# Gate tables summed by adding DMAs instead of one-hot products, in a PEER layer kernel

## The chip, the cores and the metric

One core of a Trainium2 chip runs the kernel. The metric is the device time of one execution in microseconds, from the first to the last instruction on the slowest core (there is only one). Less is better.

## What is computed

One layer of a streaming encoder on 256 tokens of width 2048, in float32: a mixer (chunked attention, a gated short convolution, gates), a cross attention, and a PEER feed-forward, each behind an RMSNorm and added to the residual, and a last norm. The change is in the PEER part:

```python
q = (h @ w_pq).reshape(bsz, seq, PEER_HEADS, 2, PEER_HALF)
s = jnp.einsum('bshpd,hpkd->bshpk', q, sub_keys)
s1, i1 = lax.top_k(s[:, :, :, 0], PEER_TOPK)          # 16 of 128 keys, 8 heads
s2, i2 = lax.top_k(s[:, :, :, 1], PEER_TOPK)
cand = s1[..., :, None] + s2[..., None, :]             # 256 candidates
top_s, pos = lax.top_k(cand, PEER_TOPK)                # expert = i1 * 128 + i2
gates = jax.nn.softmax(top_s, axis=-1)
# per token, over 8 x 16 chosen experts e of 16384:
#   out += gelu(h . expert_u[e]) * gate * expert_v[e]
```

Several heads of one token may choose the same expert; their gates then add up.

## The kernel before

Every product of the kernel streams a weight matrix in 1 MB pieces, the **tiles** of this text (`order`, in `plan`). SyncE loads a piece (`raw`, 2 buffers, line 162), ScalarE rounds it to its high half (`whi`, line 175), VectorE subtracts to get the low half (`wlo`, line 183), and TensorE multiplies both halves (`gemm_f`, lines 279 and 282). `take` fetches the halves of a tile and starts the next loads; after each tile `run_side` (line 202) hands out side work in the order in which it will stand on the engines: entries of `bulk` up to a credit of 2.75 us per tile, then the tile's `wlo`, then one entry of `chain`, then all of `late`. All engines work their instructions in this order, so what stands ahead of a `wlo` on VectorE, or ahead of a `raw` load on SyncE, holds it back.

PEER runs so. During `w_pq` (16 tiles) the key scores are made (line 1047) and `key_top` picks 16 keys, for both blocks of 128 tokens in turn. During `expert_u` (128 tiles, 16384 experts) the activations h . expert_u go to a DRAM table `ag_d` (and `tail_d` for the last 512 experts), and beside it the routing is worked off from `bulk`:

- `start_route`, `cand_top`, `gates`, `rows`, `rows_sum` of block 0, then of block 1, pick the 16 experts of each head and their gates. In `rows` the one-hot product is on GpSimd (line 756).
- `sel_t` transposes choices and gates; then for every 8 tokens `one_hot` makes one-hot rows (lines 784 and 786, low halves on ScalarE at line 791), and `gate_rows` multiplies them on TensorE (line 802, 16 products of 128x128 for 8 tokens, 512 in all), so that the products hold the summed gates, [128 first keys x 128 second keys] per token. They are staged in `gst` (line 808) and stored to `ag_d` on SyncE's queue in runs of 32 tokens (line 814). `mark` (lines 829 and 831) takes the maximum of them over tokens, per expert.
- `list_members` to `list_indices` make from the marks a list of the experts that any token chose, for both blocks or one. This takes products as well (line 934).

The last part multiplies `expert_v`. It takes the rows in the list (`list_rows`, line 961: an indirect DMA issued by GpSimd that fetches 128 rows of 8 KB) and their entries of `ag_d` (`list_gates`, line 970), and four whole tiles for the tail. The row of the final gain is loaded on SyncE's queue ahead of all loads of that part that stand behind `early.close()` (line 1119); its tile lies where tiles of the part before lay.

Of the kernel before, what the change touches and what calls it, by code (L numbers as in the profile page):

```python
# [30 lines left out]
TB = 32  # L31
# [9 lines left out]
FORCE_GENERAL = False  # L41
# [68 lines left out]
def kernel(ctx: ExitStack, tc: tile.TileContext, ap, out):  # L110
# [15 lines left out]
    tail_d = dram.tile([ND * P, NB, 2, P], F32, name="tail_d")  # L126
    xt_d = dram.tile([P, NB, D], F32, name="xt_d")
# [15 lines left out]
    order = plan()  # L143
    first_v = len(order) - len(list_order())
# [57 lines left out]
    def run_side():  # L202

        state["credit"] = min(state["credit"], 0.0) + state["slot"] if bulk else 0.0
        while bulk and state["credit"] > 0:
            cost, f = bulk.pop(0)
            state["credit"] -= cost
            if f is None:
                break
            f()  # L210
        split_low()
        if chain:
            chain.pop(0)()
        while late:
            late.pop(0)()
# [321 lines left out]
    with tc.tile_pool(name="gate", bufs=2, side="right") as gp:  # L537
        for j in range(KD):
# [141 lines left out]
    sel_i = peerc.tile([P, 2, T], F32, name="sel_i")  # L680
    sel_g = peerc.tile([P, T, 2], F32R, name="sel_g")
# [58 lines left out]
    def rows(b, which):  # L740
# [3 lines left out]
        if which == 0:  # L744
            nc.vector.tensor_single_scalar(pos, st["bi"], 4, op=ALU.logical_shift_right)
        else:
            nc.vector.tensor_single_scalar(pos, st["bi"], 15, op=ALU.bitwise_and)
# [8 lines left out]
        nc.gpsimd.tensor_tensor(eq, eq, tab.unsqueeze(2).to_broadcast(shape), op=ALU.mult)  # L756
# [5 lines left out]
    def sel_t(b):  # L762
        ps = psum()[:, 0].rearrange("p (j k) -> p j k", k=P)
        for j in range(3):
            nc.tensor.transpose(ps[:, j], route[b]["sel"][:, j].rearrange("p h k -> p (h k)"), ident)
        s = slice(b * P, (b + 1) * P)
        nc.scalar.activation(sel_i[:, :, s], ps[:, 0:2], AF.Copy)
        nc.scalar.activation(sel_g[:, s, 0], ps[:, 2], AF.Copy)
        nc.vector.tensor_sub(sel_g[:, s, 1], ps[:, 2], sel_g[:, s, 0].bitcast(F32))
# [6 lines left out]
    HK = NK // 2  # L776

    def one_hot(t0):
        i = t0 // OB % 2
        p1 = slot(f"b{2 * i}", "p1", [P, 2, OB, NK], F32R)  # L780
        p2 = slot(f"b{2 * i + 1}", "p2", [P, OB, 2, NK], F32R)
        shape = [P, OB, NK]
        for w in range(2):
            nc.vector.tensor_tensor(p1[:, w], iota.unsqueeze(1).to_broadcast(shape),
                                    sel_i[:, w, t0:t0 + OB].unsqueeze(2).to_broadcast(shape), op=ALU.is_equal)
        nc.vector.tensor_mul(p2[:, :, 0], p1[:, 0].bitcast(F32),
                             sel_g[:, t0:t0 + OB, 0].bitcast(F32).unsqueeze(2).to_broadcast(shape))

        def lows():
            for o in range(OB):  # L790
                nc.scalar.activation(p2[:, o, 1], p1[:, 0, o].bitcast(F32), AF.Copy,
                                     scale=sel_g[:, t0 + o, 1:2].bitcast(F32))

        late.append(lows)
        stage["p", t0] = p1, p2

    def gate_rows(t0):
        p1, p2 = stage.pop(("p", t0))
        ps = psum().rearrange("p a (t k) -> p (a t) k", k=NK)
        for o in range(OB):  # L800
            for w in range(2):
                nc.tensor.matmul(ps[:, o], p1[:, 1, o], p2[:, o, w], start=w == 0, stop=w == 1)  # L802
        tt = t0 % TB
        if tt == 0:
            stage["g"] = [slot(f"c{t0 // TB % 2 * 2 + i}", f"gst{i}", [P, HK, TB]) for i in range(2)]
        g = stage["g"]
        for i in range(2):
            nc.scalar.activation(g[i][:, :, tt:tt + OB], ps[:, :, i * HK:(i + 1) * HK].rearrange("p t i -> p i t"), AF.Copy)
        if tt == TB - OB:
            b, t1 = t0 // P, t0 % P + OB - TB  # L810

            def store(c):
                w = min(NK // 4, NL - c)
                nc.sync.dma_start(ag_v[:, c:c + w, b, 1, t1:t1 + TB], g[c // HK][:, c % HK:c % HK + w])
                if c + w == NL:
                    nc.sync.dma_start(tail_v[:, :, b, 1, t1:t1 + TB], g[1][:, HK - ND:HK])

            chain.extend([lambda c=c: store(c) for c in range(0, NL, NK // 4)])

    def mark(t0, i):  # L820

        g = stage["g"][i]
        b = t0 // P
        if "mk" not in stage:
            stage["mk"] = peer.tile([P, NB, NK], F32, name="mk", tag="scr")
            stage["mt"] = peer.tile([P, NB, NK], F32, name="mt", tag="scr")
        m, t = stage["mk"][:, b, i * HK:(i + 1) * HK], stage["mt"][:, 0, 0:HK]
        if t0 % P < TB:
            nc.vector.tensor_reduce(m, g, axis=AX.X, op=ALU.max)
        else:  # L830
            nc.vector.tensor_reduce(t, g, axis=AX.X, op=ALU.max)
            nc.vector.tensor_max(m, m, t)
# [13 lines left out]
    def list_triangles():  # L846
        row_u = peer.tile([P, PH], U32, name="row_u", tag="zu", bufs=1)
        nc.gpsimd.iota(row_u[:, 0:1], pattern=[[1, 1]], base=0, channel_multiplier=1)
        row = ls["row"] = peer.tile([P, PH], F32, name="row", tag="z")
        nc.vector.tensor_copy(row[:, 0:1], row_u[:, 0:1])  # L850
        nc.vector.tensor_scalar(row[:, 1:2], row[:, 0:1], 1.0, None, op0=ALU.add)
# [144 lines left out]

    def queue_routing():
        for b in range(NB):
            bulk.append((2.7, lambda b=b: start_route(b)))
# [7 lines left out]
            bulk.append((0.5, lambda b=b: late.append(lambda: sel_t(b))))
        bulk.append((0.8, list_triangles))
        bulk.append((3.7, lambda: one_hot(0)))
        for t0 in range(0, T, OB):  # L1010
            if t0 + OB < T:
                bulk.append((3.7, lambda t0=t0: one_hot(t0 + OB)))

            if t0 and t0 % TB == 0:
                for i in range(2):
                    bulk.append((2.3, lambda t0=t0, i=i: mark(t0 - OB, i)))
            bulk.append((0.0, lambda t0=t0: late.append(lambda: gate_rows(t0))))
        bulk.append((0.0, None))
# [278 lines left out]
```

## Time and profile before

| | us |
|---|---|
| median of 3 runs | 2423.39 (2417.14 to 2429.06) |
| the profiled execution, whole | 2431.38 |
| its span in the trace | 2429.4 |
| TensorE busy in it | 2381.2 (98%) |
| VectorE busy | 1640.0 (68%) |
| ScalarE busy | 1233.9 (51%) |
| GpSimd busy | 427.2 (18%) |

PE is TensorE, PEld its weight loads, DVE is VectorE, ACT ScalarE, POOL GpSimd, SP SyncE. A row of a group gives line, engine, operation, output and input, count, busy time and mean of one, and the idle time of the engine just ahead of it with what ended it. `expert_u` runs from about 1133 to 1936 us.

### The profile page before, as it was taken

How to read it: one execution, taken by the hardware profiler on the slowest of the kernel's cores; microseconds unless marked ns; L12 is line 12 of the kernel's file. 1: busy time of each engine (PE TensorE's matmuls, PEld its weight loads, DVE VectorE, ACT ScalarE, POOL GpSimd, SP SyncE). 2: the span in 40 equal slices, each digit the busy share in tenths (PEclk: the TensorE clock that was granted, in tenths of full speed). 3: DMA queues.
4: the chain of work that ended last, by engine and by line, in shares of the span. 5: the costliest groups of instructions: out<-in, count | busy, mean ns of one | idle time of the engine just before them, and what ended most of it. 6: DMA issues, size and time to landing. Idle time of an engine off the chain costs nothing.

```text
span 2429.4 us, 32024 instructions
## 1 busy us (share of the span) xinstructions
PE 2381.2 (98%) x13082; PEld 2057.0 (85%) x13082; DVE 1640.0 (68%) x1794; ACT 1233.9 (51%) x1442; POOL 427.2 (18%) x270
## 2 busy tenths in 40 slices
PE   8999999999999999999999999999999979999997
PEld 6888888888888888888888888888888868888886
DVE  6766655556854444768889878778677546776776
ACT  6444444445534434444444666676476435555555
POOL 2000000001300000200021100000000326887774
PEclk9999999999999999999999999999999989999998
DMA  6545555556554444555556589979966778888884
GB/s 242 185 171 191 178 201 192 183 186 223 191 191 173 165 165 168 186 195 179 208 188 213 177 210 230 229 209 227 241 196 212 263 276 321 302 316 309 306 319 150
DMA packets 243592, 526.47 MB, mean 217 GB/s; under 512 B 143473, under 2 KB 178289, under 8 KB 187890
## 3 DMA queue, kind: packets, MB, share of 16 engines
q1 hardware_dynamic: 185760, 371.24, 46.9%
q0 software_dynamic: 22720, 136.33, 15.4%
q10 hardware_dynamic: 34962, 16.82, 2.4%
q8 instruction: 104, 1.70, 0.3%
q14 instruction: 46, 0.38, 0.0%
HBM read 486.59 MB, written 37.75 MB: 216 GB/s over the span
## 4 chain that ended last, share of the span: by engine, by line
PE 87%; DMA 4%; DVE 3%; ACT 2%; issue 2%; SPq 0%; POOL 0%; ACTq 0%; POOLq 0%; DVEq 0%
PE g L279 40%; PE g L282 20%; PE acc L1124 6%; PE acc L1125 6%; PE acc L1123 6%; DMA raw<-in_expert_u_dram 3%; PE g L258 2%; PE g L259 2%; PE g L257 2%; PE t L802 2%; DVE wlo L183 2%; ACT whi L175 1%; DMA tail_d<-h 1%; PE t L603 1%; PE t L650 1%
## 5 line engine op out<-in xcount | busy, mean ns | idle before, releaser
L279 PE MATMUL g<-op_a,whi 128*128 128x512 f32 x3200 | 1009.1, 397 | 0.0
L183 DVE TENSOR_TENSOR wlo<-raw,whi 128x2048 fp32r<-128x2048 f32 x322 | 744.7, 2313 | 306.3 <-ACT whi L175 303.7
L175 ACT ACTIVATE whi<-raw 128x2048 fp32r<-128x2048 f32 x322 | 616.5, 1915 | 460.3 <-PE g L279 186.1
L282 PEld LDWEIGHTS g<-op_a,wlo 128*128 128x128 f32 x3200 | 600.8, 188 | 151.9 <-DVE wlo L183 9.8
L282 PE MATMUL g<-op_a,wlo 128*128 128x256 f32 x3200 | 631.0, 279 | 6.6 <-DVE wlo L183 6.6
L279 PEld LDWEIGHTS g<-op_a,whi 128*128 128x128 f32 x3200 | 488.1, 189 | 0.1
L183 DVE TENSOR_TENSOR wlo<-rows,whi 128x2048 fp32r<-128x2048 f32 x110 | 251.7, 2289 | 95.3 <-ACT whi L175 94.6
L175 ACT ACTIVATE whi<-rows 128x2048 fp32r<-128x2048 f32 x110 | 211.1, 1919 | 169.8 <-PE acc L1125 122.2
L961 POOL DMA_INDIRECT rows<-in_expert_v_dram,idx x110 | 161.4, 1468 | 641.7 <-PE g L282 534.3
L1123 PE MATMUL acc<-whi,es 128*128 128x512 f32 x640 | 249.1, 389 | 1.4 <-DVE h L289 1.4
L1125 PE MATMUL acc<-whi,es 128*128 128x512 f32 x640 | 249.0, 389 | 0.0
L1124 PE MATMUL acc<-wlo,es 128*128 128x512 f32 x640 | 249.0, 389 | 0.0
L279 PE MATMUL g<-op_b,whi 128*128 128x512 f32 x704 | 222.6, 397 | 0.0
L364 POOL TENSOR_TENSOR acc<-acc,sq 128x512 f32<-128x512 f32 x21 | 39.7, 1890 | 943.4 <-ACT sq L363 934.5
L970 POOL DMA_INDIRECT ag<-ag_d,idx x110 | 176.8, 1608 | 68.4 <-DMA ag_d<-h 35.2
L279 PE MATMUL g<-op_c,whi 128*128 128x512 f32 x576 | 182.9, 399 | 0.0
L282 PEld LDWEIGHTS g<-op_b,wlo 128*128 128x128 f32 x704 | 132.2, 188 | 31.2
L1123 PEld LDWEIGHTS acc<-whi,es 128*128 128x128 f32 x640 | 120.1, 188 | 26.7 <-DVE h L289 1.6
L1124 PEld LDWEIGHTS acc<-wlo,es 128*128 128x128 f32 x640 | 120.1, 188 | 24.9
L1125 PEld LDWEIGHTS acc<-whi,es 128*128 128x128 f32 x640 | 120.1, 188 | 24.9
L282 PE MATMUL g<-op_b,wlo 128*128 128x256 f32 x704 | 138.4, 278 | 0.0
L282 PEld LDWEIGHTS g<-op_c,wlo 128*128 128x128 f32 x576 | 108.2, 188 | 25.6
(260 smaller groups left out, 2428.6 us busy)
## 6 DMA issues: line engine op xcount, KB each, us to landing
raw<-in_expert_u_dram SPq DMA_DIRECT2D x128, 1024.0 KB, 5.2
raw<-in_w_in_dram SPq DMA_DIRECT2D x72, 1024.0 KB, 4.7
raw<-in_w_out_dram SPq DMA_DIRECT2D x16, 1024.0 KB, 4.8
raw<-in_w_mix_out_dram SPq DMA_DIRECT2D x16, 1024.0 KB, 4.8
raw<-in_w_ck_dram SPq DMA_DIRECT2D x16, 1024.0 KB, 4.8
raw<-in_w_cq_dram SPq DMA_DIRECT2D x16, 1024.0 KB, 4.7
raw<-in_w_cv_dram SPq DMA_DIRECT2D x16, 1024.0 KB, 4.7
raw<-in_w_co_dram SPq DMA_DIRECT2D x16, 1024.0 KB, 4.7
```

Of the source, the lines that this page charges most:

```text
L175: nc.scalar.activation(hi, raws[n], AF.Copy)
L183: nc.vector.tensor_sub(lo, raws.pop(n), halves[n][0].bitcast(F32))
L257: nc.tensor.matmul(ps[:, b], op.high(kt, b), hi[:, k], start=kt == 0, stop=False)
L258: nc.tensor.matmul(ps[:, b], op.high(kt, b), lo[:, k], start=False, stop=False)
L259: nc.tensor.matmul(ps[:, b], op.low(kt, b), hi[:, k], start=False, stop=kt == KD - 1)
L279: nc.tensor.matmul(dst, hi[:, kt], op.both(kt), start=first, stop=False)
L282: nc.tensor.matmul(dst[:, T:2 * T], lo[:, k], op.high(k), start=False, stop=last and k == kt)
L961: nc.gpsimd.indirect_dma_start(raw, None, ap["expert_v"], bass.IndirectOffsetOnAxis(ap=idx[:, 0, t:t + 1], axis=0))
L970: nc.gpsimd.indirect_dma_start(AGS[g][:, i, 0:w], None, src, bass.IndirectOffsetOnAxis(ap=idx[:, 1, t:t + 1], axis=0))
L1123: nc.tensor.matmul(acc[b][c], e_hi, hi[:, c], start=first, stop=False, skip_group_check=True)
L1124: nc.tensor.matmul(acc[b][c], e_hi, lo[:, c], start=False, stop=False, skip_group_check=True)
L1125: nc.tensor.matmul(acc[b][c], e_lo, hi[:, c], start=False, stop=last, skip_group_check=True)
```

## The change

The summed gates are no longer made by products. Two tables `gate_d` in DRAM, one for each block of tokens, are set to zero during the gate stage (16 stores of 1 MB on SyncE's queue, one after each of 16 tiles). When a block has been routed, `places` works out for each choice its element in the table, and `scatter` issues 128 indirect DMAs on GpSimd, one for each head and rank, each of which adds 128 gates (4 bytes each, one for each token) to elements of the table. The 16 DMAs of a head may run together; those of the next head wait until all 16 have landed. Behind each stands a `memset` of one element on GpSimd. Then `gates_in` loads the table back, 1 MB at a time, for `mark`, and `gates_out` copies it into `ag_d`, DRAM to DRAM. These wait until all sums of their block have landed. They are started at fixed tiles: the numbers in `MARKS_AT`, `COPIES_AT` and `XROWS_AT` count tiles before the first of `expert_v`, so that -66 is tile 62 of `expert_u` and -40 is tile 88. `gates_in` is on SyncE's queue for block 0 and on GpSimd's for block 1; `gates_out` is on SyncE's.

Beside this, block 0 is routed whole before `key_top` of block 1; the product in `rows` moves from GpSimd to VectorE; the transposes of x (`x_rows_t`) move to tiles 36 to 50; and the load of the final gain moves from the start of the `expert_v` part to behind its last whole tile.

```diff
+gate_d = [dram.tile([P, NK, P], F32, name=f"gate_d{b}") for b in range(NB)]
...
+MARKS_AT = (-66, -40)
+COPIES_AT = (-60, -28)
+COPY_STEP = (2, 1)
+XROWS_AT = -92
...
@@ run_side @@
         if chain:
             chain.pop(0)()
+        for f in timed.pop(state["use"] - first_v, []):
+            f()
         while late:
...
@@ gate stage @@
+        none = gp.tile([P, KC, P], F32, name="none", bufs=1)
+        nc.gpsimd.memset(none, 0.0)
+        chain += [lambda b=b, c=c: nc.sync.dma_start(gate_d[b][:, c:c + KC], none)
+                  for b in range(NB) for c in range(0, NK, KC)]
...
@@ rows @@
+        if which:
+            low = peer.tile([P, PH, TOPK], F32, name="low", tag="scr")[:, :, :]
+            nc.vector.tensor_copy(low, st["bi"])
+            nc.vector.scalar_tensor_tensor(posf, posf, -float(TOPK), low, op0=ALU.mult, op1=ALU.add)
...
-        nc.gpsimd.tensor_tensor(eq, eq, tab.unsqueeze(2).to_broadcast(shape), op=ALU.mult)
+        nc.vector.tensor_tensor(eq, eq, tab.unsqueeze(2).to_broadcast(shape), op=ALU.mult)
...
-    def sel_t(b):
...
-    def one_hot(t0):
...
-    def gate_rows(t0):
...
+    def places(b):
+        sel = route[b]["sel"]
+        at = peer.tile([P, PH * TOPK], F32, name="at", tag="posf", bufs=1)
+        i1, i2 = [sel[:, w].rearrange("p h k -> p (h k)") for w in range(2)]
+        nc.vector.scalar_tensor_tensor(at, i2, float(NK), i1, op0=ALU.mult, op1=ALU.add)
+        nc.vector.tensor_scalar(at, at, float(P), row[:, 0:1], op0=ALU.mult, op1=ALU.add)
+        place = route[b]["place"] = peer.tile([P, PH * TOPK], U32, name="place")
+        nc.vector.tensor_copy(place, at)
+
+    def scatter(b):
+        table = gate_d[b].rearrange("i k t -> (i k t)").unsqueeze(1)
+        g = route[b]["sel"][:, 2].rearrange("p h k -> p (h k)")
+        before = []
+        for h in range(PH):
+            key = f"head{b}{h}"
+            now = []
+            for c in range(h * TOPK, (h + 1) * TOPK):
+                ins = nc.gpsimd.indirect_dma_start(
+                    table, bass.IndirectOffsetOnAxis(ap=route[b]["place"][:, c:c + 1], axis=0), g[:, c:c + 1], None,
+                    compute_op=ALU.add).ins
+                if now:
+                    tc.declare_no_dep(ins, group=key, reason="a head's choices are all different")
+                for i in before:
+                    tc.add_manual_dep(ins, i.name, SUMS, reason="another head may have chosen the same expert")
+                tc.add_to_no_dep_group(key, ins)
+                now.append(ins)
+                nc.gpsimd.memset(row_u[0:1, 1:2], 0)
+            before = now
+        route[b]["last"] = before
...
+    def gates_in(n):
+        b, c = divmod(n, NK // KC)
+        g = stage[n] = slot(f"c{n % 4}", "gst", [P, KC, P])
+        ins = (nc.gpsimd if b else nc.sync).dma_start(g, gate_d[b][:, c * KC:(c + 1) * KC]).ins
+        for i in route[b]["last"]:
+            tc.add_manual_dep(ins, i.name, SUMS, reason="all sums of the table")
+
+    def gates_out(b, k):
+        parts = [(ag_v[:, k:min(k + 8, NL), b, 1], gate_d[b][:, k:min(k + 8, NL)])]
+        if k + 8 > NL:
+            parts.append((tail_v[:, :, b, 1], gate_d[b][:, NL:NK]))
+        for dst, src in parts:
+            ins = nc.sync.dma_start(dst, src).ins
+            for i in route[b]["last"]:
+                tc.add_manual_dep(ins, i.name, SUMS, reason="all sums of the table")
+
+    def mark(n):
+        b, c = divmod(n, NK // KC)
...
+        nc.vector.tensor_reduce(stage["mk"][:, b, c * KC:(c + 1) * KC], stage[n], axis=AX.X, op=ALU.max)
...
@@ queue_routing @@
         for b in range(NB):
+            if b:
+                bulk.extend(tops)
...
+            bulk.append((0.8, lambda b=b: places(b)))
+            bulk.append((0.0, lambda b=b: scatter(b)))
+        for i in range(NB * KD // 4):
+            timed.setdefault(XROWS_AT + 2 * i, []).append(lambda i=i: late.append(lambda: x_rows_t(*divmod(i, KD // 4))))
+        for b in range(NB):
+            timed.setdefault(MARKS_AT[b], []).append(lambda b=b: queue_marks(b))
+            for i in range(KD):
+                timed.setdefault(COPIES_AT[b] + i * COPY_STEP[b], []).append(lambda b=b, i=i: gates_out(b, 8 * i))
+
+    def queue_marks(b):
+        n0 = b * NK // KC
+        for n in range(NK // KC + 2):
+            if n < NK // KC:
+                bulk.append((0.0, lambda n=n: late.append(lambda: gates_in(n0 + n))))
+            if n >= 2:
+                bulk.append((2.3, lambda n=n: mark(n0 + n - 2)))
+            bulk.append((0.0, None))
+        if b == 0:
+            bulk.append((0.8, list_triangles))
+            return
         bulk.append((1.3, list_members))
...
@@ key_scores @@
-                for b in range(NB):
-                    bulk.append((1.6, lambda b=b, hp=hp: key_top(b, hp)))
+                bulk.append((1.6, lambda hp=hp: key_top(0, hp)))
+                tops.append((1.6, lambda hp=hp: key_top(1, hp)))
...
@@ last part @@
     gain = fin.tile([P, D // CW, CW], F32, name="gain")
-    nc.sync.dma_start(gain.rearrange("p c w -> p (c w)"), ap["gain_row"].to_broadcast([P, D]))
...
         if v == last_whole:
+            nc.sync.dma_start(gain.rearrange("p c w -> p (c w)"), ap["gain_row"].to_broadcast([P, D]))
             x_tok = x_load_t()
```

## Rows read from the trace of the kernel before

**Rows 1.** The page: busy time of each engine, share of the span, instructions.

```profile
PE 2381.2 (98%) x13082; PEld 2057.0 (85%) x13082; DVE 1640.0 (68%) x1794; ACT 1233.9 (51%) x1442; POOL 427.2 (18%) x270
```

**Rows 2.** Busy time by stretch: length, engines (instructions), PE clock, DMA share, GB/s.

```profile
1133.00:1936.00 803.00, 795.88 (x4801) 701.54 (x4799) 632.14 (x747) 459.66 (x682) 44.23 (x17) 1.00 0.74 214
1250.00:1350.00 100.00, 95.03 (x536) 82.01 (x535) 91.05 (x115) 45.72 (x40) 26.29 (x5) 0.98 0.53 181
1460.00:1560.00 100.00, 99.57 (x623) 88.54 (x623) 79.11 (x59) 62.55 (x111) 0.00 (x0) 1.00 0.91 225
1945.00:1967.00 22.00, 8.54 (x38) 6.75 (x36) 2.35 (x3) 1.70 (x1) 5.26 (x6) 0.81 1.02 425
1967.00:1975.00 8.00, 6.20 (x14) 4.53 (x15) 7.50 (x7) 4.32 (x5) 2.59 (x1) 0.50 0.46 167
```

**Rows 3.** The chain of waits, in order of time: start us, us, what.

```profile
1126.78 0.89 PE t L1047 x8
1138.82 0.89 PE t L1047 x8
...
1370.57 1.74 PE t L802 x16
```

**Rows 4.** Groups of TensorE's instructions by line: the one-hot products.

```profile
L802 PE MATMUL t<-p,p 128*128 128x128 f32 x512 | 60.7, 272 | 0.0
```

**Rows 5.** GpSimd in order of time, last part: start us, us, instruction, idle before.

```profile
2096.25 0.95 POOL L970 DMA_INDIRECT ag<-ag_d,idx  x1 [0.30 <-issue]
...
2098.76 2.98 POOL L961 DMA_INDIRECT rows<-in_expert_v_dram,idx  x1 [0.30 <-DVE ag L984]
2102.05 2.43 POOL L961 DMA_INDIRECT rows<-in_expert_v_dram,idx  x1 [0.30 <-issue]
2104.78 0.94 POOL L961 DMA_INDIRECT rows<-in_expert_v_dram,idx  x1 [0.30 <-issue]
```

**Rows 6.** VectorE over the same stretch.

```profile
2098.64 2.28 DVE L183 TENSOR_TENSOR wlo<-rows,whi 128x2048 fp32r<-128x2048 f32 x1
...
2101.38 2.28 DVE L183 TENSOR_TENSOR wlo<-rows,whi 128x2048 fp32r<-128x2048 f32 x1
...
2105.16 2.29 DVE L183 TENSOR_TENSOR wlo<-rows,whi 128x2048 fp32r<-128x2048 f32 x1 [0.95 <-ACT whi L175]
```

**Rows 7.** VectorE in a quiet stretch at the same pace of tiles.

```profile
715.77 2.29 DVE L183 TENSOR_TENSOR wlo<-raw,whi 128x2048 fp32r<-128x2048 f32 x1 [2.55 <-ACT whi L175]
...
722.06 2.29 DVE L183 TENSOR_TENSOR wlo<-raw,whi 128x2048 fp32r<-128x2048 f32 x1 [0.39 <-ACT whi L175]
726.91 2.29 DVE L183 TENSOR_TENSOR wlo<-raw,whi 128x2048 fp32r<-128x2048 f32 x1 [2.56 <-ACT whi L175]
```

**Rows 8.** The tile `ag`, 1915 to 1960 us: its indirect DMAs' time from issue to landing.

```profile
DMA to landing us min/median/max: 2.9/3.6/17.6
```

**Rows 9.** Groups by line: ScalarE's rounding, GpSimd's product in `rows`, a small memset.

```profile
L175 ACT ACTIVATE whi<-raw 128x2048 fp32r<-128x2048 f32 x322 | 616.5, 1915 | 460.3 <-PE g L279 186.1
...
L756 POOL TENSOR_TENSOR eq<-eq,topf 128x2048 f32<-128x2048 f32 x4 | 26.2, 6550 | 203.1 <-DVE eq L753 203.1
L431 POOL MEMSET cu<- 128x2 f32 x2 | 0.1, 96 | 0.0
```

**Rows 10.** SyncE's issues, then TensorE, from `expert_u` to `expert_v`, in order of time.

```profile
1913.80 0.94 SPq L1069 DMA_DIRECT2D wg<-tail_d  x2
1952.28 0.35 SPq L1119 DMA_DIRECT2D gain<-in_gain_row_dram  x1
1952.68 22.22 SPq L162 DMA_DIRECT2D raw<-in_expert_v_dram  x4
...
1967.26 0.79 PE L1123 MATMUL acc<-whi,we 128*128 128x512 f32 x1 [13.73 <-ACT whi L175]
1969.59 0.79 PE L1124 MATMUL acc<-wlo,we 128*128 128x512 f32 x1 [1.53 <-DVE wlo L183]
```

**Rows 11.** DMA issues by line: KB of one, median us from issue to landing.

```profile
raw<-in_w_in_dram SPq DMA_DIRECT2D x72, 1024.0 KB, 4.7
```

More of the change, by code (lines that the diff above doesn't have):

```diff
@@ L30 @@
 ET = NE // P
-TB = 32
+KC = 16
+MARKS_AT = (-66, -40)
+COPIES_AT = (-60, -28)
+COPY_STEP = (2, 1)
+XROWS_AT = -92
 ND = 4
@@ L143 @@
     order = plan()
+    timed = {}
     first_v = len(order) - len(list_order())
@@ L549 @@
                 put_split_later(MG, j - 1, 2, ma)
+        drain_chain()
         settle()
@@ L679 @@
     topi = [peerc.tile([P, 2 * PH, TOPK], U32, name=f"topi{b}") for b in range(NB)]
-    sel_i = peerc.tile([P, 2, T], F32, name="sel_i")
-    sel_g = peerc.tile([P, T, 2], F32R, name="sel_g")
+    row_u = peerc.tile([P, PH], U32, name="row_u")
+    nc.gpsimd.iota(row_u[:, 0:1], pattern=[[1, 1]], base=0, channel_multiplier=1)
+    row = peerc.tile([P, PH], F32, name="row")
+    nc.vector.tensor_copy(row[:, 0:1], row_u[:, 0:1])
+    nc.vector.tensor_scalar(row[:, 1:2], row[:, 0:1], 1.0, None, op0=ALU.add)
     NEG = -3.0e38
@@ L730, in gates @@
         bs = st["bs"]
-        sel = st["sel"] = peer.tile([P, 3, PH, TOPK], F32, name="sel", bufs=1)
+        sel = st["sel"] = peer.tile([P, 3, PH, TOPK], F32, name="sel")
         g = sel[:, 2]
@@ L743, in rows @@
         pos = peer.tile([P, PH, TOPK], U32, name="pos", bufs=1)
[L744 to L747, printed above, removed]
+        nc.vector.tensor_single_scalar(pos, st["bi"], 4, op=ALU.logical_shift_right)
         posf = peer.tile([P, PH, TOPK], F32, name="posf", bufs=1)
         nc.vector.tensor_copy(posf, pos)
+        if which:
+            low = peer.tile([P, PH, TOPK], F32, name="low", tag="scr")[:, :, :]
+            nc.vector.tensor_copy(low, st["bi"])
+            nc.vector.scalar_tensor_tensor(posf, posf, -float(TOPK), low, op0=ALU.mult, op1=ALU.add)
         tab = st["topf"].rearrange("p (h a) k -> p h a k", a=2)[:, :, which, :]
@@ L760, in rows_sum @@
         nc.vector.tensor_reduce(route[b]["sel"][:, which], route[b]["eq", which], axis=AX.X, op=ALU.add)
-    def sel_t(b):
[L763 to L769, printed above, removed]
+    def places(b):
[26 more added lines that the diff above has]
+        route[b]["last"] = before
     ag_v = ag_d[0:NM].rearrange("(e p) b a t -> p e b a t", p=P)
@@ L775 @@
     OB = 8
-    HK = NK // 2
-    def one_hot(t0):
[L779 to L795, printed above, removed]
@@ L797, in gate_rows @@
-    def gate_rows(t0):
[L798 to L818, printed above, removed]
@@ L839, in list_members @@
         mk = stage["mk"]
-        m3 = ls["m"] = peer.tile([P, 3, P], F32, name="m3", tag="sel", bufs=1)
+        m3 = ls["m"] = peer.tile([P, 3, P], F32, name="m3", tag="sel")
         nc.vector.tensor_single_scalar(mk, mk, 0.0, op=ALU.is_gt)
@@ L846, in list_triangles @@
     def list_triangles():
[L847 to L851, printed above, removed]
+        ls["row"] = row
         ge = ls["ge"] = peer.tile([P, P], F32, name="ge", tag="bs", bufs=1)
@@ L1003, in queue_routing @@
             for w in range(2):
-                bulk.append((2.8, lambda b=b, w=w: rows(b, w)))
+                bulk.append((5.0, lambda b=b, w=w: rows(b, w)))
             for w in range(2):
                 bulk.append((2.3, lambda b=b, w=w: rows_sum(b, w)))
[L1007 to L1018, printed above, removed]
-        for i in range(2):
-            bulk.append((2.3, lambda i=i: mark(T - OB, i)))
+            bulk.append((0.8, lambda b=b: places(b)))
[17 more added lines that the diff above has]
+            return
         bulk.append((1.3, list_members))
@@ L1033, in queue_routing @@
             bulk.append((0.0, lambda c=c: late.append(lambda: list_rows_add(c))))
-            if c % (2 * OB) == 0:
-                bulk.append((0.0, lambda c=c: late.append(lambda: x_rows_t(*divmod(c // (2 * OB), KD // 4)))))
         bulk.append((0.0, None))
```

12 lines of the change are left out of this document (2 added, 10 removed).

## The prediction, made before the run

> **What bounds the kernel now.** I read the page's busy times first: TensorE is busy for 2381.2 of 2429.4 us [rows 1]. So only TensorE's work and its few pauses count, and the next view is the one by stretches. From 1133 to 1936 us, all of `expert_u`, TensorE is busy for 795.88 of 803 us; of the 7 us lost, 4.97 lie between 1250 and 1350 us, where VectorE is at 91% and GpSimd works at the product in `rows` [rows 2]. In the chain a tile takes its own time and side products add to it: the key scores of the last two heads start 12.04 us apart, two tiles and one set of 0.89 us, so a tile lasts (12.04 - 0.89) / 2 = 5.575 us, and the last set stands right behind tile 0, which places the end of tile k, without gate products, at 1139.7 + 5.575 k [rows 3]. A pause that stands out lies where `expert_v` begins: TensorE waits 13.73 and 1.53 us for the halves of the first whole tile [rows 10].
>
> **What is removed.** There are 512 one-hot products in groups of 16 [rows 4]. Their busy time of 60.7 us overlaps at both ends; in the chain a group takes 1.74 us [rows 3], so 32 x 1.74 = 55.7 us leave TensorE, with six transposes of `sel_t` at 0.11 (1.74 / 16) another 0.7. All of it lies on the path, since TensorE doesn't pause there. The pause of 4.97 us goes too: VectorE's sums waited for GpSimd's product of 6.55 us [rows 9], and on VectorE the product is one more pass over 128x2048, about 2.3 us as a `wlo` [rows 7], four in all, budgeted in the new 5.0. Routing then fills VectorE to 2.29 + 2.75 = 5.0 of 5.575 us a tile, additions of `h` aside; I take the pause as gone, at worst it stays. One-hot rows on VectorE and ScalarE and the `gst` stores go as well, but nothing waited for them: -61.4 us.
>
> **The gain's load.** On SyncE's queue it is issued at 1952.28, after 38 us in which SyncE issued nothing, and the four whole tiles come behind it [rows 10]; TensorE waits for the first. Moved, it leaves these loads free to go once their buffers are, near 1920. The pause of 13.73 + 1.53 us goes, and with it most of the 8 us behind it in which the granted clock was 0.50, the lower level, after the idle stretch [rows 2]; half of that is 4 us. What could be late next is a row of the list: in the pause the DMA engines ran at share 1.02 and 425 GB/s [rows 2]. That traffic is some 10 MB of prefetch, needed only one MB every 2.7 to 5.5 us. I take -18, between -19 and -8. At its new place the load is behind all whole tiles, and only the end waits for it, 400 us later.
>
> **Small additions.** The 16 stores of zeros put a second MB into each of 16 tiles. A load lands in 4.7 us [rows 11]; with another MB at 425 GB/s [rows 2] ahead of it that is 7.2, and with `whi` (1.9) [rows 9] and `wlo` (2.29) [rows 7] a buffer is taken for 11.4 us, where two tiles give 11.15. So 16 x 0.13 = 2 us, from 0 to 6; nothing there can shrink. `gates_in` does the same in 16 tiles: 2 us, 0 to 6. `gates_out` moves what the `gst` stores moved, in longer runs, and with those the DMA share was 0.91 while TensorE lost 0.43 of 100 us [rows 2]: 0. Transposes of x cost the same where they go, and the order of `key_top` costs nothing.
>
> Without waits the sum is -61.4 - 18 + 4, about **-75 us**.
>
> **The scatter, which decides.** It needs GpSimd, 256 times. An indirect DMA of 128 rows holds GpSimd for 0.95 us with 0.30 to the next; rows of 8 KB (L961) and of 1 or 2 KB (L970) cost the same [rows 5], so I take the number of rows as the price, and 0.95 for 128 gates too. That an addition costs more isn't excluded by any row. The memset is 0.10 [rows 9]; it may lie in the gap of 0.30 or lengthen it to 0.4 or 0.6.
>
> But a DMA whose start falls into a `wlo` waits. The one at 2098.76 starts 0.12 us into a `wlo` and takes 2.98, until 0.8 to 0.9 behind that `wlo`'s end; the one at 2102.05 starts within the next `wlo` (2101.38 to 2103.66) and ends at 2104.48; the one at 2104.78 begins ahead of a `wlo` and takes 0.94 [rows 5, 6]. In the quiet stretch, and so behind the routing, two tiles hold `wlo`s at 0 and at 4.85 (or 6.30) us [rows 7]. Between them 2.56 and 4.01 us are free. With a pitch of 1.25 the blocked DMA ends 0.9 behind the `wlo`, and starts fall at 1.20 and 2.45, then at 1.20, 2.45 and 3.70. That is 3 + 4 = **7 DMAs in 11.15 us, 1.59 each**. With 1.35 to 1.4 the starts at the edges are lost by turns: 6 or 5 in two tiles, 1.86 or 2.23 each. The lower bound, no `wlo` at all, is 1.25. I take 1.59, as no row shows that a memset without a wait adds to the gap.
>
> The Trainium skill (SBUF — State Buffer, "Who interferes with whom") says that a VectorE instruction with two SBUF inputs contends with a GpSimd instruction that reads SBUF, and that whichever issues first has the shared pair for the whole instruction. By that a DMA that began first would hold back `wlo`, up to 0.95 us a tile; in tiles 17 to 41, where VectorE has some 0.5 us left in each, the sum would be up to 24 x 0.45 = 11 us worse. This trace disagrees for `wlo`: the one at 2105.16 begins 0.38 us into a DMA and takes 2.29, as in the quiet stretch [rows 5 to 7].
>
> Between heads the first DMA waits until the 16 before have landed: 3.6 us from issue at the median [rows 8], less its own 0.95, and a start of 0.30, so 3.0 (2.3 by the shortest). A head is 16 x 1.59 + 3.0 = **28.5 us**; without `wlo`s, 16 x 1.35 + 3.0 = 24.6.
>
> When does it start? The queue of side work, counted off at 2.75 us a tile, reaches block 0's `start_route` at tile 4 and `scatter` 37.7 / 2.75 tiles on, at tile 17: 1235 us. Block 0 ends at 1235 + 8 x 28.5 = 1463. Its `gates_in` follow tile 62, about 1489 (with 3.5 us for the transposes of x). So SyncE, which has all later `raw` loads behind that wait, isn't held. Block 1 runs on from 1463. Its `gates_in` stand on GpSimd behind its own DMAs, which harms no load, but `mark` stands on VectorE after tile 90 ahead of the `wlo` of tile 92, and waits. TensorE ends tile 91 at 1651. By 1648 there are 185 / 28.5 = 6.5 heads done; VectorE then stands still, so the last 1.5 take 24.6 each: done at 1685. Loading a table piece (4.7, and 1 to issue it), `mark` (2.3) and `wlo` (2.3) make 1696. **TensorE stands for 45 us**, and list work follows in its old order, ending three tiles later against `expert_v` than before, at tile 120; its first user comes at 124.
>
> Sum: -75 + 45 = **-30 us**. The profiled execution took 2431.4, 8.0 above the median of the three, so 2401 by the profile and **2393** as a median.
>
> **Rivals.**
> 1. *The scatter keeps up.* If a DMA with its share of waits costs 1.39 us or less, 256 are done by 1640 and nothing waits: -75, **2348**. For it: 1.25 without `wlo`s. Against it: every `wlo` holds one DMA. Eight in two tiles would do.
> 2. *Six in two tiles.* A head takes 16 x 1.86 + 3.0 = 32.8 us. Block 0 ends at 1498, SyncE is held some 6 us, and block 1 ends near 1734 (4.8 heads by 1655, 3.2 at 24.6): TensorE stands for 87 us more. -75 + 93 = +18: **2441**. The change breaks even at a head of 31 us, 1.76 a DMA.
> 3. *Slower: the DMA is dearer.* Five in two tiles, or an addition that takes GpSimd 1.5 us. A head takes 38.7 us, block 0 would end at 1545. SyncE stands at `gates_in` from 1489, TensorE from about 1500 to 1537; block 1 ends near 1791 and costs 113 more: -75 + 150 = +75, **2498**. The same happens if the DMA engines take long over single additions of 4 bytes; the trace has no such packet.
>
> That the tables aren't what the products gave would change no time here.
>
> **How the numbers follow.** Forecast 0.36, keeping up 0.24, six in two tiles 0.20, dearer 0.20. The forecast's own range, 2365 to 2418, goes by a head of 27 to 30 us and the small bounds. From 2340 to 2465 leaves out most of the dearer cases and the edge of rival 1: some 0.18. A measurement can tell about 0.5%, 12 us. Faster by more (below 2411): 0.24 + 0.33 + 0.01 = 0.58; slower by more (above 2435.5): 0.20 + 0.08 = 0.28; between: 0.14.
>
> **What the profile will show.** No product of `gate_rows`; no wait of 13 us at the first whole tile; the mean of GpSimd's adding DMA, and its pitch against `wlo`; a wait of `mark` 8 on its table piece, of some 50 us. SyncE held at `gates_in` 0 would mean a dearer scatter. Wrong would be the forecast if the adding DMA holds GpSimd for other than 0.95 us, if the memset moves the pitch over an edge, or if landing takes far longer than 3.6 us.

## The result, and the profile after

Beside runs of the kernel before with a median of 2426.22 us (2417.14 to 2432.29, four runs), the changed kernel took 2560.86 us (2560.09 to 2566.75, four runs): a ratio of 1.0563 [1.0525, 1.0602]. It is 134.6 us **slower**; forecast were 2393 us, with 2465 as the upper end. The profiled execution after took 2566.75 us, with a span of 2565.0 us. In the code after, the adding DMA is L802, the memset behind it L811, `gates_in` L825, `gates_out` L835, `mark` L845; the lines of `wlo`, `whi` and the two products of `g` are L192, L184, L293 and L290.

The page after, its first rows (as in [rows 1]) and the slices of TensorE, GpSimd and the granted clock, 64 us each:

```profile
PE 2327.8 (91%) x12564; PEld 2003.5 (78%) x12564; DVE 1525.1 (59%) x1698; ACT 1127.1 (44%) x1118; POOL 914.0 (36%) x787
...
PE   8999999999999999999999964980089999999997
...
POOL 2000000003100001100578777877700055788774
PEclk9999999999999999999999987995599999999998
```

TensorE's busy time fell by 53.4 us against [rows 1], so the products did leave it. But its time without work rose from 48.2 us (2429.4 - 2381.2) to 237.2 us (2565.0 - 2327.8), by 189.0. The difference of the spans is 189.0 - 53.4 = 135.6 us. The slices say where: two gaps, at slices 23 to 24 and 27 to 28 (counted from 0), both while GpSimd is 70% busy or more. The granted clock sinks to 0.5 in the second, the lower of its two levels.

Which wait makes the gaps stands in the view of waits, from 1480 to 1900 us of the kernel after (waiter, what it waited for, total us, times, longest us):

```profile
DVE mk L845 <- DMA gst<-gate_d: 207.1, 3, 148.4
...
PE g L293 <- DVE wlo L192: 148.5, 5, 142.7
...
PE g L290 <- ACT whi L184: 53.5, 2, 52.8
```

and in what SyncE issues (first fence) and VectorE does (second) around the two gaps, in order of time:

```profile
1465.34 27.48 SPq L171 DMA_DIRECT2D raw<-in_expert_u_dram  x6
1559.51 0.33 SPq L825 DMA_DIRECT2D gst<-gate_d  x1
```

```profile
1564.38 2.29 DVE L845 TENSOR_REDUCE mk<-gst 128x16 f32<-128x2048 f32 x1 [57.89 <-DMA gst<-gate_d]
...
1860.90 2.29 DVE L845 TENSOR_REDUCE mk<-gst 128x16 f32<-128x2048 f32 x1 [148.38 <-DMA gst<-gate_d]
1863.10 2.28 DVE L192 TENSOR_TENSOR wlo<-raw,whi 128x2048 fp32r<-128x2048 f32 x1
```

The first gap: SyncE's issues of `raw` end at 1492.8 (1465.34 + 27.48), then nothing goes out until 1559.51, when block 0's table is complete and its first `gates_in` is let go. The loads of `raw` stand behind it, so TensorE stands 52.8 us for `whi`. The second: VectorE waits 148.38 us at `mark` 8 for the first piece of block 1's table, the next `wlo` stands behind it at 1863.10, and TensorE waits 142.7 us for that. Together 195.5 us. Both waits end where the scatter ends, so the scatter's pace is the question. Its group (page), and a stretch of it in which all else stands still (GpSimd in order of time; start us, us, instruction, idle before it):

```profile
L802 POOL DMA_INDIRECT gate_d<-sel,place x256 | 479.3, 1872 | 238.1 <-DVE top L704 116.2
...
L811 POOL MEMSET row_u<- 1x1 uint32 x256 | 158.3, 618 | 0.0
```

```profile
1730.07 1.56 POOL L802 DMA_INDIRECT gate_d<-sel,place  x1 [0.27 <-issue]
1731.06 0.61 POOL L811 MEMSET row_u<- 1x1 uint32 x1
1731.93 1.56 POOL L802 DMA_INDIRECT gate_d<-sel,place  x1 [0.27 <-issue]
```

With nothing beside it, one DMA starts 1.86 us after another (1731.93 - 1730.07; the **pitch**), where the prediction had 1.25, and up to 1.4 with the memset in the gap. Beside the tiles, the first six heads of block 0, from 1243, took 38.6 to 43.5 us each; block 0 ended near 1557 and block 1 at 1855. Forecast were 28.5 us a head and 1463 for block 0.

The rest of the change's places. Stretches of the kernel after (columns as in [rows 2]): the place of the old pause in the routing, the stores of zeros in two widths, and the step to `expert_v`; below them the wider stretch of the stores in the kernel before, and the products of the first whole tiles of `expert_v` in the kernel after.

```profile
1250.00:1350.00 100.00, 100.00 (x577) 87.33 (x576) 87.37 (x212) 45.58 (x39) 82.18 (x77) 1.00 0.71 205
...
300.00:400.00 100.00, 94.95 (x524) 82.03 (x523) 47.25 (x37) 38.22 (x33) 0.00 (x0) 0.97 0.98 327
...
290.00:410.00 120.00, 113.18 (x618) 97.63 (x617) 59.95 (x49) 49.50 (x43) 1.81 (x1) 0.96 0.90 304
...
2060.00:2110.00 50.00, 48.12 (x252) 40.97 (x251) 30.45 (x30) 26.11 (x26) 24.65 (x17) 1.00 0.87 324
```

```profile
290.00:410.00 120.00, 120.00 (x691) 104.68 (x690) 68.70 (x53) 55.53 (x48) 0.00 (x0) 1.00 0.55 193
```

```profile
L1140 PE MATMUL acc<-whi,we 128*128 128x512 f32 x32 | 12.4, 389 | 0.0
L1141 PE MATMUL acc<-wlo,we 128*128 128x512 f32 x32 | 12.4, 389 | 0.0
```

The pause of 4.97 us in the routing is gone (100.00 of 100, before 95.03, [rows 2]), and so are the 13.73 and 1.53 us at the first whole tile of `expert_v` [rows 10]: its products show no idle time. New is a loss where the zeros are stored, 6.8 us from 290 to 410 (120.00 - 113.18), of which 5 lie between 300 and 400 with the DMA engines at share 0.98; before, TensorE was busy there throughout.

### The profile page after: what moved, and what is told of

It is laid out like the page before. It is cut to its first block, busy times and chain, and to the rows that moved or that the text cites. A ratio compares the mean times of both kernels' runs of the same rounds, so it can differ in the third digit from the quotient of the medians.

```text
span 2565.0 us, 31232 instructions
## 1 busy us (share of the span) xinstructions
PE 2327.8 (91%) x12564; PEld 2003.5 (78%) x12564; DVE 1525.1 (59%) x1698; ACT 1127.1 (44%) x1118; POOL 914.0 (36%) x787
## 4 chain that ended last, share of the span: by engine, by line
PE 65%; POOL 18%; DMA 9%; issue 4%; DVE 2%; ACT 2%; POOLq 0%; SPq 0%; ACTq 0%; DVEq 0%
PE g L290 27%; POOL gate_d L802 18%; PE g L293 13%; PE acc L1140 6%; PE acc L1142 6%; PE acc L1141 6%; DMA gate_d<-sel,place 3%; DMA raw<-in_w_in_dram 2%; DMA raw<-in_expert_u_dram 2%; DVE wlo L192 2%; PE g L269 2%; PE g L270 2%; PE g L268 2%; ACT whi L184 1%; DMA raw<-in_w_out_dram 1%
## 5 line engine op out<-in xcount | busy, mean ns | idle before, releaser
L290 PE MATMUL g<-op_a,whi 128*128 128x512 f32 x3200 | 1013.7, 398 | 59.1 <-ACT whi L184 53.5
L192 DVE TENSOR_TENSOR wlo<-raw,whi 128x2048 fp32r<-128x2048 f32 x322 | 737.7, 2291 | 383.0 <-ACT whi L184 377.8
L184 ACT ACTIVATE whi<-raw 128x2048 fp32r<-128x2048 f32 x322 | 616.5, 1914 | 674.2 <-DMA raw<-in_expert_u_dram 351.4
L293 PEld LDWEIGHTS g<-op_a,wlo 128*128 128x128 f32 x3200 | 604.5, 189 | 294.5 <-DVE wlo L192 151.7
L293 PE MATMUL g<-op_a,wlo 128*128 128x256 f32 x3200 | 633.0, 279 | 148.5 <-DVE wlo L192 148.5
L802 POOL DMA_INDIRECT gate_d<-sel,place x256 | 479.3, 1872 | 238.1 <-DVE top L704 116.2
L290 PEld LDWEIGHTS g<-op_a,whi 128*128 128x128 f32 x3200 | 490.8, 190 | 60.6 <-ACT whi L184 54.3
L192 DVE TENSOR_TENSOR wlo<-rows,whi 128x2048 fp32r<-128x2048 f32 x110 | 251.7, 2289 | 93.7 <-ACT whi L184 92.2
L184 ACT ACTIVATE whi<-rows 128x2048 fp32r<-128x2048 f32 x110 | 211.0, 1919 | 167.8 <-PE acc L1142 119.6
L970 POOL DMA_INDIRECT rows<-in_expert_v_dram,idx x110 | 176.4, 1604 | 238.1 <-DVE idx L958 170.7
L290 PE MATMUL g<-op_b,whi 128*128 128x512 f32 x704 | 222.6, 397 | 0.0
L290 PE MATMUL g<-op_c,whi 128*128 128x512 f32 x576 | 182.8, 399 | 0.0
L845 DVE TENSOR_REDUCE mk<-gst 128x16 f32<-128x2048 f32 x16 | 36.5, 2279 | 207.1 <-DMA gst<-gate_d 207.1
L811 POOL MEMSET row_u<- 1x1 uint32 x256 | 158.3, 618 | 0.0
L293 PEld LDWEIGHTS g<-op_b,wlo 128*128 128x128 f32 x704 | 132.2, 188 | 32.8 <-DVE wlo L192 1.6
L1140 PEld LDWEIGHTS acc<-whi,es 128*128 128x128 f32 x640 | 120.1, 188 | 26.9 <-DVE h L300 2.1
```

What stands on the lines that cost most here:

```text
L184: nc.scalar.activation(hi, raws[n], AF.Copy)
L192: nc.vector.tensor_sub(lo, raws.pop(n), halves[n][0].bitcast(F32))
L290: nc.tensor.matmul(dst, hi[:, kt], op.both(kt), start=first, stop=False)
L293: nc.tensor.matmul(dst[:, T:2 * T], lo[:, k], op.high(k), start=False, stop=last and k == kt)
L802: ins = nc.gpsimd.indirect_dma_start(table, bass.IndirectOffsetOnAxis(ap=route[b]["place"][:, c:c + 1], axis=0), g[:, c:c + 1], None, comp ...
L811: nc.gpsimd.memset(row_u[0:1, 1:2], 0)
```

## The experiments

The question after the result: is the pace of 1.86 us that of the memset (0.61 where 0.10 was taken), of the addition, or of something else that any scatter would pay? And how much of the 39 to 43 us a head is `wlo`'s doing? Then the small terms, and last a version by the prices found. The kernel before had a median of 2427.24 us beside the runs without and with two memsets, with the gain's load alone and with the zeros alone, and 2428.84 beside the other four.

### No memset

```
-                nc.gpsimd.memset(row_u[0:1, 1:2], 0)
+                nc.gpsimd.nop(nofuse=True)
```

> The changed kernel with a sequencer no-op in place of each of the 256 memsets. In the changed kernel an adding DMA starts every 1.86 us when nothing holds it: the memset begins 0.98 us after the DMA, takes 0.61, and 0.27 later the next DMA begins. Theory A, the memset is what was priced wrong (0.10 forecast, 0.61 measured, in line and not in the gap): the DMA itself holds GpSimd 0.95 to 1.0 us as a gather does, the unheld pitch falls to 1.25 to 1.35, a head beside the wlo takes about 30 us in place of 39.5, TensorE's stands shrink from some 196 us to 40 to 80, and the kernel takes 2395 to 2450 us. Theory B, an addition itself holds GpSimd 1.56 us and the memset only waits out its tail: the pitch stays at 1.8 to 1.9 and the time within 2540 to 2565.

Measured: 2559.64 us (2554.64 to 2565.4), ratio 1.0546 [1.0523, 1.0568]. GpSimd in order of time, while all else stands still:

```profile
1729.56 1.55 POOL L802 DMA_INDIRECT gate_d<-sel,place  x1 [0.30 <-issue]
1731.41 1.55 POOL L802 DMA_INDIRECT gate_d<-sel,place  x1 [0.30 <-issue]
1733.27 1.55 POOL L802 DMA_INDIRECT gate_d<-sel,place  x1 [0.30 <-issue]
```

The pitch is 1.85 to 1.86 us without any memset, and the time is the same. The memset isn't the cause. In the kernel after it starts 0.99 us into the DMA (1730.07 to 1731.06) and ends 0.04 us behind it: its 0.61 us lie within the DMA's 1.56.

### Two memsets

```
                 nc.gpsimd.memset(row_u[0:1, 1:2], 0)
+                nc.gpsimd.memset(row_u[0:1, 1:2], 0)
```

> The changed kernel with a second memset behind each of the 256. If a memset costs 0.6 us of its own, the unheld pitch goes from 1.86 to about 2.4 to 2.5 us, and the time rises by 256 x 0.6 less what the wlos hide, some 80 to 150 us, to 2640 to 2710. If the first memset only waits for the tail of the DMA ahead of it, the second costs about 0.1 us as an ordinary small memset: pitch 1.95 to 2.05, time up by 10 to 35 us.

Measured, in one run: 2564.53 us, within the range of the kernel after. GpSimd in order of time, nothing beside it:

```profile
1738.83 1.56 POOL L802 DMA_INDIRECT gate_d<-sel,place  x1 [0.16 <-issue]
1739.81 0.61 POOL L811 MEMSET row_u<- 1x1 uint32 x1
1740.48 0.09 POOL L812 MEMSET row_u<- 1x1 uint32 x1
1740.73 1.56 POOL L802 DMA_INDIRECT gate_d<-sel,place  x1 [0.15 <-issue]
```

The second memset takes 0.09 us, as a small memset did before (96 ns for 128x2 elements, [rows 9]), and the pitch grows by 0.04 to 1.90, less than the 0.1 to 0.2 expected; the time doesn't rise by the 10 us and more that were expected. Of the two theories the second holds: the first memset's 0.61 is the wait for the DMA's last part, not work. A memset between DMAs costs next to nothing: it lies in the gap, as the prediction had it.

### The scatter without the addition

The DMA stores its gates in place of adding them, so gates that several choices send to one place overwrite each other; number, size and places of the DMAs are the same.

```
-                    table, bass.IndirectOffsetOnAxis(ap=route[b]["place"][:, c:c + 1], axis=0), g[:, c:c + 1], None,
-                    compute_op=ALU.add).ins
+                    table, bass.IndirectOffsetOnAxis(ap=route[b]["place"][:, c:c + 1], axis=0), g[:, c:c + 1], None).ins
```

> The changed kernel with plain writes in place of additions: the 256 indirect DMAs overwrite their elements, so a gate of another head or of nothing is not added up. All else, waits too, is the same. Theory A, the addition is dear: GpSimd is held 0.95 to 1.0 us as by a gather of 128 rows, the unheld pitch falls from 1.86 to 1.25 to 1.4, a head beside the wlo to some 30 us, and the time to 2395 to 2450 us. Theory B, a scatter of 128 elements of 4 bytes costs 1.55 us whether it adds or not: pitch 1.8 to 1.9, time 2545 to 2565. A price in between would go by interpolation: each 0.1 us of the 1.55 is worth some 20 to 26 us of time.

Measured, in one run: 2419.01 us, 142 below the kernel after. GpSimd in order of time, then VectorE in the same stretch:

```profile
1275.11 0.96 POOL L802 DMA_INDIRECT gate_d<-sel,place  x1 [0.21 <-issue]
1276.08 0.09 POOL L810 MEMSET row_u<- 1x1 uint32 x1
1276.38 2.23 POOL L802 DMA_INDIRECT gate_d<-sel,place  x1 [0.21 <-issue]
1278.60 0.09 POOL L810 MEMSET row_u<- 1x1 uint32 x1
1278.91 0.96 POOL L802 DMA_INDIRECT gate_d<-sel,place  x1 [0.23 <-issue]
```

```profile
1275.50 2.27 DVE L192 TENSOR_TENSOR wlo<-raw,whi 128x2048 fp32r<-128x2048 f32 x1
```

and its waits from 1450 to 1900 us (columns as above):

```profile
DVE mk L844 <- DMA gst<-gate_d: 65.6, 1, 65.6
...
PE g L293 <- DVE wlo L192: 61.5, 2, 59.9
```

This settles the price. A scatter of 128 gates of 4 bytes holds GpSimd for 0.96 us at a pitch of 1.27 (1276.38 - 1275.11), as rows of 1 to 8 KB did [rows 5]; **the addition costs 0.6 us more**. At the plain price the prediction's picture holds: the DMA that starts within a `wlo` waits until 0.84 us behind its end (1276.38 + 2.23 - 1277.77), SyncE isn't held, VectorE stands at `mark` 8, and TensorE stands 60 us. Its numbers were still too low: the heads of block 0 take 27.2 to 37.7 us, 30.7 on average, where 28.5 were worked out, and TensorE's stand was put at 45.

### No `wlo` on VectorE

`wlo` of `expert_u`'s tiles is made on ScalarE as a copy of the load instead of the difference, so that one VectorE instruction with two SBUF operands leaves each tile.

```
-            nc.vector.tensor_sub(lo, raws.pop(n), halves[n][0].bitcast(F32))
+            if order[n][0] == "expert_u":
+                nc.scalar.activation(lo, raws.pop(n), AF.Copy)
+            else:
+                nc.vector.tensor_sub(lo, raws.pop(n), halves[n][0].bitcast(F32))
```

> The changed kernel with the low half of each tile of expert_u made on ScalarE, as a copy of the tile and not as a difference, so that VectorE has no wlo in that stage. In the changed kernel a head takes 39.5 us beside the wlo and 31.9 without. If it is the wlo that holds the DMAs, a head takes 32 to 34.5 us from the first on, block 0 ends near 1510 and not 1559, TensorE stands some 120 us and not 196, and the time is 2470 to 2500 us. If something else in that stretch holds them (loads, DMA traffic), heads stay at 38 to 40 us and the time at 2550 to 2570.

Measured, in one run: 2477.58 us, 83 below the kernel after. The group of the adding DMA (columns as on the page), its code here at L805:

```profile
L805 POOL DMA_INDIRECT gate_d<-sel,place x256 | 403.1, 1575 | 232.1 <-DVE top L707 114.1 <-issue 65.1 <-DMA gate_d<-sel,place 52.6
```

and a wait of TensorE from 1450 to 1900 us:

```profile
PE g L293 <- DVE h L303: 103.2, 1, 103.2
```

The mean falls from 1872 to 1575 ns, close to the undisturbed 1560, and the first five heads take 32.7, 33.0, 32.5, 37.2 and 33.8 us, where they took 43.5, 43.0, 43.4, 42.4 and 38.6 in the kernel after. So `wlo` accounts for 10 to 11 us of each of the first three heads and some 5 of the next two. The first stand of TensorE is all but gone (4.9 us from 1490 to 1610), and the second, behind `mark` 8, is down to 103.2 us. The head of 37.2 shows that `wlo` isn't alone in this: four of its DMAs start within the passes of `rows` over 128x2048 with two inputs (`eq`, 2.29 us), and each ends 1.43 to 1.44 us behind that pass. The prediction counted `wlo` only. How `wlo` holds a DMA shows in these rows of the kernel after, GpSimd first:

```profile
1444.75 1.56 POOL L802 DMA_INDIRECT gate_d<-sel,place  x1 [0.27 <-issue]
...
1446.61 2.69 POOL L802 DMA_INDIRECT gate_d<-sel,place  x1 [0.27 <-issue]
```

```profile
1445.58 2.29 DVE L192 TENSOR_TENSOR wlo<-raw,whi 128x2048 fp32r<-128x2048 f32 x1 [2.57 <-ACT whi L184]
```

The first DMA began ahead of `wlo` and isn't stretched; the second starts within it and ends at 1449.30, 1.43 us behind `wlo`'s end at 1447.87. A plain one ends 0.84 behind: the addition is paid after the wait. The Trainium skill (SBUF — State Buffer, "Who interferes with whom") says that a VectorE instruction with two SBUF inputs contends with a GpSimd instruction that reads SBUF, and, of VectorE's two-port modes, that whoever issues first gets the shared pair for the whole instruction. The trace agrees with such an order for a DMA that comes second, and not for a `wlo` that does: this one begins 0.83 us into a DMA and takes 2.29 us, as in [rows 7].

### Half of the scatter

Of the 16 DMAs of each head eight are issued, and half of the gates left out.

```
-            for c in range(h * TOPK, (h + 1) * TOPK):
+            for c in range(h * TOPK, h * TOPK + TOPK // 2):
```

> The changed kernel with 8 of the 16 DMAs of each head, so half of the gates are left out of the tables; all waits, loads and copies are the same. If the stands of TensorE come from the number of DMAs times their price, a head takes 8 x 2.25 + 3.7 = 21.7 us, block 0 ends near 1417 and block 1 near 1590, ahead of the tiles that wait for them, and no stand is left: 2427 less 56 for the products, 16 for the gain and 5 for the product in rows, plus 12 for the zeros and 0 to 4 for the table loads: 2360 to 2370 us. Rival: the loads and copies of the tables, or the waits themselves, also cost: over 2385.

Measured: 2358.18 us (2353.77 to 2364.66), ratio 0.9719 [0.9702, 0.9736]. The scatter ran from 1240 to 1606 us, heads of 18 to 28 us, and the stretch that held the first gap reads:

```profile
1490.00:1610.00 120.00, 120.00 (x691) 104.72 (x690) 73.38 (x43) 53.73 (x44) 80.59 (x78) 1.00 0.99 316
```

TensorE doesn't stand there at all. With the scatter in time, the change saves 71 us (2428.84 - 2358.18; 2 us less than the lower end of the time expected); the prediction's sum without waits was 75. So the rest of the change makes the kernel faster, and the scatter's lateness makes it slower.

### The gain's load alone

The kernel before, with only the gain's load moved behind the last whole tile:

```
-    nc.sync.dma_start(gain.rearrange("p c w -> p (c w)"), ap["gain_row"].to_broadcast([P, D]))
...
+            nc.sync.dma_start(gain.rearrange("p c w -> p (c w)"), ap["gain_row"].to_broadcast([P, D]))
```

> The kernel before with the load of the final gain moved behind the last whole tile, and nothing else. The forecast gave this step -18 us, between -19 and -8: the waits of 13.73 and 1.53 us at the first whole tile go. Expected 2400 to 2416 us, ratio about 0.9925. Rival: the rows of the list are late instead, and nothing or under 5 us is won.

Measured: 2411.28 us (2409.36 to 2413.49), ratio 0.9931 [0.9918, 0.9945]: 16.0 us less, where 18 were forecast. The two waits at the first whole tile are gone here too.

### The zeros alone

The kernel before, with only the 16 stores of zeros:

```
+    gate_d = [dram.tile([P, NK, P], F32, name=f"gate_d{b}") for b in range(NB)]
...
+        none = gp.tile([P, 16, P], F32, name="none", bufs=1)
+        nc.gpsimd.memset(none, 0.0)
+        chain += [lambda b=b, c=c: nc.sync.dma_start(gate_d[b][:, c:c + 16], none)
+                  for b in range(NB) for c in range(0, NK, 16)]
```

> The kernel before with the 16 stores of zeros, 1 MB each, added to the gate stage, and nothing else (the tables are not used). The forecast gave them +2 us, from 0 to 6. In the changed kernel TensorE loses 5 us between 300 and 400 us and 1.8 us between 400 and 535 us, which would make +6 to +8. Rival: the loss there comes from somewhere else in the change, and this kernel is within 2 us of the kernel before.

Measured: 2439.11 us (2438.41 to 2443.75), ratio 1.0045 [1.0031, 1.0058]: 11.9 us more, where the prediction had 2 and the expectation 6 to 8. The stretch of the stores:

```profile
300.00:400.00 100.00, 90.88 (x512) 77.32 (x511) 47.36 (x37) 37.16 (x33) 0.00 (x0) 1.00 0.96 317
```

With a load and a store of one MB to each tile the DMA engines are taken at share 0.96, and they move 317 GB/s, not 425 as in [rows 2]. Two MB then take 2 x 1.049 MB / 317 GB/s = 6.6 us, and a tile has 5.575 [rows 3]. From 290 to 410 us TensorE loses 10.9 us here, and 6.8 in the kernel after; why the same stores cost less there wasn't taken apart.

### One block by the scatter, one by products

From 1232 us to tile 78, near 1600, there are some 46 us for each of eight heads, and a head costs 38.6 to 43.5: so all of block 0 is done before anything needs it, and block 1's gates come from the one-hot products as before. The marks of block 0 are asked for 50 tiles before `expert_v`, its copies from 48 on at every second tile; eight stores of zeros remain, one to every second tile; the gain's load is at its new place.

```
-    gate_d = [dram.tile([P, NK, P], F32, name=f"gate_d{b}") for b in range(NB)]
+    gate_d = [dram.tile([P, NK, P], F32, name="gate_d0")]
...
+        for c in range(0, NK, KC):
+            chain += [lambda c=c: nc.sync.dma_start(gate_d[0][:, c:c + KC], none), lambda: None]
...
+            if b == 0:
+                bulk.append((0.8, lambda b=b: places(b)))
+                bulk.append((0.0, lambda b=b: scatter(b)))
+            else:
+                bulk.append((0.5, lambda b=b: late.append(lambda: sel_t(b))))
```

> A kernel of both kinds: block 0 by the scatter, with its table loaded from tile 78 on, block 1 by one-hot products as before the change, 8 stores of zeros spread over 16 tiles, and the gain's load at its new place. 128 DMAs at the measured 39.5 us a head end near 1560, ahead of tile 78 at about 1600, so nothing waits; 16 of 32 groups of products go, 16 x 1.74 = 28 us, the gain gives 16, the zeros cost 0 to 4. Expected 2378 to 2392 us, faster than the kernel before by 1.5 to 2%. Rival: the scatter of block 0 runs later beside the one-hot work of VectorE and SyncE is held again: 2410 or more.

Measured: **2382.34 us** (2379.13 to 2386.38), ratio 0.981 [0.9797, 0.9823]. Its tile `gate_d` (count: shortest, median, longest ns; first and last start), and the stretch of its stores of zeros:

```profile
L814 POOL DMA_INDIRECT gate_d<-sel,place x128: 1556/1902/3647, 1232.4 to 1570.9; - x128
```

```profile
290.00:400.00 110.00, 110.00 (x633) 95.97 (x632) 64.05 (x50) 50.86 (x44) 1.81 (x1) 1.00 0.78 268
```

The scatter ends near 1575, ahead of the first `gates_in` at 1611, and nothing stands for it. Eight stores of zeros, one to every second tile, cost TensorE nothing there (110.00 of 110 us). This version is faster than both kernels: 46.5 us below the one before, of which the gain's load accounts for 16.0 by the run above.

## Why the prediction was wrong

**The step that failed** is the price of one adding DMA: "so I take the number of rows as the price, and 0.95 for 128 gates too". No row of before had an addition, the prediction said that "an addition costs more isn't excluded by any row", and it still took the value without. Without addition the same DMA does hold GpSimd for 0.96 us; with it, 1.56. The pitch is then 1.86, not 1.25, and the edges that the prediction drew by 1.25 between two `wlo`s give fewer places. Repeating that count with the measured rows: a DMA that was blocked ends 1.43 us behind `wlo`, the next starts 0.27 later at 1.70, and the one after that at 3.56. In the free stretch of 2.56 us [rows 7] that leaves two DMAs, in the one of 4.01 three. Five in 11.15 us are 2.23 each, and 16 x 2.23 + 3.8 (the landing, 56.9 us over 15 waits) = 39.5 us; eight of the sixteen heads took 38.6 to 43.5, and one 47.1. That is past the 31 us at which the prediction saw the change break even.

The count itself was a little short even at the plain price: with 0.96 us a DMA a head of block 0 took 30.7 us and not 28.5. The count of seven needs DMAs that start 0.11 and 0.31 us ahead of a `wlo`, and it leaves out the passes of `rows` that hold a DMA as `wlo` does.

**What the extra time did** was foreseen as the third rival, down to its place: SyncE held from about 1489 (measured 1493), TensorE standing until the first table is done, and VectorE at `mark` 8. Its time of 2498 was still 63 us too low. Its stands came to 150 us and measured 195.5, since block 0 ended some 12 us later than its 1545 and block 1 some 64 later than its 1791. The rival's 38.7 us a head were near the truth beside the tiles, but its 1791 goes by 24.6 us a head during the stand, at a pitch of 1.35, which an addition of 1.5 us doesn't allow; the last four heads measured 31.7 to 32.1. The zeros make up another 5 (6.8, not 2), and shorter waits around the stands some 7. So the mechanism was priced, but given one chance in five where its condition, a dearer addition, was the thing no row spoke to.

**The other terms**, against the runs:
- Products and transposes, -56.4 forecast: TensorE's busy time fell by 53.4. Right to 3 us.
- The pause in the routing, -5: it is gone, 100.00 of 100 us busy.
- The gain's load, -18: measured -16.0 by itself. Right.
- The zeros, +2 (0 to 6): +11.9 by itself and 6.8 in the kernel after, out of its bounds both times. The term was mis-sized as it took 425 GB/s of another stretch, and summed the latencies of one tile's buffer. The traffic fits better: two MB a tile take 6.6 us at the 317 GB/s measured, for tiles of 5.575. That it is the traffic is argued; no run tests it by itself.
- `gates_in` and `gates_out`, +2 and 0: not measured apart. With the scatter out of the way (half of it left out) the whole change gives -71 with the zeros in it, so the two together are small.
- SyncE "isn't held" at `gates_in` 0: wrong, by the same step; with a plain scatter it is right.
- The memset in the gap: right, though in another way. It looks like 0.61 us, most of which is waiting for the DMA in front.
- The landing between heads, 3.0: measured 3.8.

Put together: from 1490 to 1940 us TensorE is without work for 204.5 us, where it was for 2.2 before (1490 to 1936). With 6.8 for the zeros, less 5.0 in the routing and 15.3 at `expert_v`, that is 188.8 of the 189.0 us by which its idle time rose; with 53.4 us of work gone, the spans should differ by 135.4, and differ by 135.6. Of the 204.5, the two stands are 195.5. The other 9 are shorter waits around them, which weren't taken apart; what the granted clock of 0.50 during the stands costs behind them lies in the busy time and wasn't either.

Without the addition the kernel is 142 us faster (2560.86 - 2419.01), with `wlo` out of the DMAs' way 83 (2560.86 - 2477.58). Neither alone takes the stands away: 60 us are left in the one case and 103 in the other. The two effects overlap, so they don't add up, and no run has both.

## What to carry to other kernels

An operation that is issued 256 times and of which the trace has no row is worth measuring before anything else is worked out: here 0.6 us each decided between 2419 and 2561 us, more than all other terms of the sum together. Count an engine's DMAs at their pitch beside the work that blocks them, not at their duration in a quiet stretch, and hold the sum against the first in-order queue (here SyncE's loads, then VectorE's `wlo`) that will stand behind the result. And where a replacement is too slow to finish in time, let it do as much as fits: half of the gates through the scatter, half through products, beats either.

## What the hardware showed that was not expected

- An indirect DMA of 128 elements of 4 bytes holds GpSimd 0.96 us when it stores and 1.56 us when it adds, without anything beside it.
- A memset right behind an adding DMA shows 0.61 us, a second one behind it 0.09: a small instruction's duration can be the tail of what stands ahead of it. Behind a plain DMA it shows 0.09 at once.
- An indirect DMA that starts within a `wlo` ends 0.84 us behind it if it stores and 1.43 if it adds; one that started ahead of `wlo` isn't stretched (1.56), and `wlo` isn't either (2.29). Other passes of VectorE over 128x2048 with two inputs hold an adding DMA in the same way (1.43 to 1.44 behind their end).
- Where 1 MB stores of zeros ran beside 1 MB loads, the DMA engines were at share 0.96 to 0.98 and moved 317 to 327 GB/s; in the pause before `expert_v`, with loads only, share 1.02 went with 425. What makes the difference isn't shown.
